# Gate and up products of two feed-forward layers as seven block products for eight

## The chip, the cores and the metric

The kernel runs on one core of one Trainium2 chip. The metric is the device time of one execution in microseconds (us). Each kernel runs several times; the median counts. The engines are called as the profile calls them: PE is TensorE (matmuls; PEld is its weight load), DVE is VectorE, ACT is ScalarE, POOL is GpSimd, and SP is SyncE, which issues the transfers.

## The reference: a two-layer trunk

Activations are 512 tokens by 1024 features in float32. Layer 0 mixes the tokens with multi-head latent attention, layer 1 with a gated linear recurrence. Around the mixer every layer does the same:

```
x <- LayerNorm(alpha * x + mixer(x))
x <- LayerNorm(alpha * x + SwiGLU(x))
x <- x + sigmoid(x W_gate[i]) * (p[i] W_proj[i])

def swiglu_ffn(x, w_in, w_down):
    h = x @ w_in                                # [512, 1024] @ [1024, 2 * 2816]
    g, u = h[..., :D_FF], h[..., D_FF:]         # D_FF = 2816 = 22 * 128
    return (jax.nn.silu(g) * u) @ w_down
```

The change concerns `x @ w_in`, the gate and up products, once in each layer.

## The kernel before, in words

**Exact products in three passes.** Every large operand is split into hi + lo (`split`, L104): ACT copies it to hi with fewer significant bits (L106), and DVE, or POOL where asked, subtracts hi from it to get lo (L107). `mm3` (L118) then issues three matmuls: hi·hi (L121), hi·lo (L122) and lo·hi (L123). A matmul takes 128 rows of contraction, 128 output features and as many columns as its name in the profile says. Weights come once from memory in units of 512 KB, a tile of 128 × 1024 (`unit`, L109: tiles `raw`, `whi`, `wlo`).

**Gate and up (`ffn`, L303).** D_FF is cut into 22 blocks of 128 features. For block j the unit of gate weights and that of up weights, 8 chunks of contraction each, go through `mm3` with all 512 tokens: 2 × 8 × 3 = 48 matmuls of 512 columns. ACT applies Silu to the gate bank (L315) and DVE multiplies it by the up bank (L316). Blocks 0 and 1 are done in two halves of 256 tokens: first both blocks for token tiles 0 and 1, then both for tiles 2 and 3. That is so because the activations are not ready yet.

**What stands ahead of it.** The mixer's output projection (`out_proj`, L289) makes x token tile by token tile (four tiles of 128 tokens), in two halves of 512 features. In the second half each tile's residual (L250), layer norm statistics (L256, L257, the Square on ACT at L258), the power on POOL (`rr`, L131) and two scaling steps (L263, L267) follow its matmuls; `flush` then transposes an earlier tile on PE (L227, bank `tp`) and splits it into the feature-major pair xT. The work of one tile is issued behind the matmuls of the next.

**What stands behind it.** `hT` holds the 22 blocks' results; the down projection splits one block of hT and one unit of weights at a time (`hsplit`, tiles `ma`), and multiplies into eight PSUM banks (`part`).

**What sets the order.** The code's text order is not the engines' order: a scheduler places each engine's instructions in one fixed list before the run, by tile pools and dependences. An engine works through its list in order, and an instruction that waits holds up all behind it. Tiles come from pools with a fixed number of buffers (`mid`: tags `ma`, 4 buffers, and `mb`, 5; `raw` 3, `whi` and `wlo` 5 each), and taking one again waits for its last reader. Large tiles come from `bigt`, six of 16 KB per partition.

Of the kernel before, what the change touches and what calls it, by code (L numbers as in the profile page):

```python
# [71 lines left out]


class Builder:
    def __init__(self, ctx, tc, ins, out):
# [19 lines left out]
    def bigt(self, shape, dt=F32):  # L95
        return self.big.tile(shape, dt, tag="big", name=self.nm("big"))
# [21 lines left out]
    def mm3(self, ps, a, b, start, stop):  # L118
        """ps += a^T b with (hi, lo) operands."""
        mm = self.nc.tensor.matmul  # L120
        mm(ps, a[0], b[0], start=start, stop=False)  # L121
        mm(ps, a[0], b[1], start=False, stop=False)  # L122
        mm(ps, a[1], b[0], start=False, stop=stop)  # L123
# [97 lines left out]
    def to_feat(self, src, dst, t, c0, n):  # L221
        """chunks c0..c0+n of src [128 tok, n*128] into dst hi/lo [128, chunk, tok]"""
        for g in range(0, n, 4):
            m = min(4, n - g)
            ps = self.bank("tp")
            for c in range(m):
                self.nc.tensor.transpose(out=ps[:, c * P:(c + 1) * P], in_=src[:, (g + c) * P:(g + c + 1) * P], identity=self.ident)  # L227
            sl = (slice(None), slice(c0 + g, c0 + g + m), slice(t * P, (t + 1) * P))
            self.split(dst[0][sl], dst[1][sl], ps.rearrange("p (c t) -> p c t", t=P)[:, :m])
# [592 lines left out]
```

## Time and profile before

| | |
|---|---|
| runs | 1330.73 to 1331.20 us, median 1331.07 |
| profiled execution | span 1329.1 us (its own time is not recorded apart from the span; the median of the runs lies 1.97 above it) |
| PE busy | 1305.8 us, 98% of the span |
| DVE, ACT, POOL busy | 640.2, 463.4, 85.6 us |
| gate/up of layer 0, first to last matmul | 187.28 to 430.88 us on the span's clock |
| moved by DMA | 124.74 MB, 94 GB/s on average |

How to read it: a line such as `L107 DVE TENSOR_TENSOR wlo<-raw,whi 128x1024 ... x195 | 240.3, 1235 | 261.5 <-ACT whi L106 256.9` is a group of 195 instructions of source line 107 on DVE that read `raw` and `whi` and write `wlo`; they were busy for 240.3 us, 1235 ns each on average; DVE was idle for 261.5 us just ahead of them, most of it until ACT's L106 was done. In a timeline the first two numbers are start and duration in us, and a bracket at the end is the idle time ahead. A clock of 1.00 is full speed for PE.

### The profile page before, as it was taken

How to read it: one execution, taken by the hardware profiler on the slowest of the kernel's cores; microseconds unless marked ns; L12 is line 12 of the kernel's file. 1: busy time of each engine (PE TensorE's matmuls, PEld its weight loads, DVE VectorE, ACT ScalarE, POOL GpSimd, SP SyncE). 2: the span in 40 equal slices, each digit the busy share in tenths (PEclk: the TensorE clock that was granted, in tenths of full speed). 3: DMA queues.
4: the chain of work that ended last, by engine and by line, in shares of the span. 5: the costliest groups of instructions: out<-in, count | busy, mean ns of one | idle time of the engine just before them, and what ended most of it. 6: DMA issues, size and time to landing. Idle time of an engine off the chain costs nothing.

```text
span 1329.1 us, 16105 instructions
## 1 busy us (share of the span) xinstructions
PE 1305.8 (98%) x6460; PEld 1094.5 (82%) x6460; DVE 640.2 (48%) x1068; ACT 463.4 (35%) x760; POOL 85.6 (6%) x87
## 2 busy tenths in 40 slices
PE   8999999999999999999999999999999999999998
PEld 8787889888888888788888887888888888888887
DVE  7988373322223333753367776456322222333473
ACT  6666243222222222542434344334222222233252
POOL 0200130000000000100002220023000000000000
PEclk9999989999999999999999999999999999999999
DMA  7212133233222222241311110314223232222221
GB/s 254 77 51 96 51 108 96 96 99 101 100 95 95 95 95 95 85 152 64 126 65 64 64 65 19 125 64 138 101 95 98 98 102 99 95 95 95 95 96 48
DMA packets 35932, 124.74 MB, mean 94 GB/s; under 512 B 4369, under 2 KB 4625, under 8 KB 35729
## 3 DMA queue, kind: packets, MB, share of 16 engines
q1 hardware_dynamic: 35856, 123.71, 27.9%
q8 instruction: 51, 0.84, 0.3%
q14 instruction: 25, 0.20, 0.0%
HBM read 121.60 MB, written 2.10 MB: 93 GB/s over the span
## 4 chain that ended last, share of the span: by engine, by line
PE 92%; DVE 5%; issue 1%; ACT 1%; POOL 1%; DMA 0%; SPq 0%; DVEq 0%; ACTq 0%; POOLq 0%
PE ps L122 24%; PE ps L121 24%; PE ps L123 23%; PE sc L121 2%; PE sc L122 2%; PE sc L123 2%; PE tp L121 2%; PE tp L122 2%; PE tp L123 2%; PE tp L227 2%; PE sc L658 2%; PE wg L122 1%; PE wg L123 1%; DVE big L267 1%; PE wg L121 1%
## 5 line engine op out<-in xcount | busy, mean ns | idle before, releaser
L106 ACT ACTIVATE whi<-raw 128x1024 fp32r<-128x1024 f32 (+1 forms) x215 | 224.0, 1043 | 438.3 <-PE ps L122 325.9
L107 DVE TENSOR_TENSOR wlo<-raw,whi 128x1024 fp32r<-128x1024 f32 (+1 forms) x203 | 246.4, 1216 | 262.5 <-ACT whi L106 257.9
L121 PE MATMUL ps<-big,whi 128*128 128x512 f32 (+1 forms) x928 | 351.4, 379 | 0.0
L123 PE MATMUL ps<-big,wlo 128*128 128x512 f32 (+1 forms) x928 | 350.6, 378 | 0.0
L122 PE MATMUL ps<-big,whi 128*128 128x512 f32 (+1 forms) x928 | 349.4, 377 | 0.0
L123 PEld LDWEIGHTS ps<-big,wlo 128*128 128x128 f32 x928 | 175.9, 190 | 30.5
L122 PEld LDWEIGHTS ps<-big,whi 128*128 128x128 f32 x928 | 176.0, 190 | 30.1
L121 PEld LDWEIGHTS ps<-big,whi 128*128 128x128 f32 x928 | 176.1, 190 | 29.4
L121 PE MATMUL ps<-whi,big 128*128 128x512 f32 (+2 forms) x440 | 171.0, 389 | 0.2 <-DVE ma L453 0.2
L123 PE MATMUL ps<-whi,big 128*128 128x512 f32 (+2 forms) x440 | 168.7, 383 | 0.0
L122 PE MATMUL ps<-wlo,big 128*128 128x512 f32 (+2 forms) x440 | 168.4, 383 | 0.0
L316 DVE TENSOR_TENSOR big<-ps,t 128x512 f32<-128x512 f32 (+1 forms) x48 | 31.1, 647 | 148.5 <-PE ps L123 148.5
L123 PEld LDWEIGHTS ps<-whi,big 128*128 128x128 f32 x440 | 83.1, 189 | 15.6
L121 PEld LDWEIGHTS ps<-whi,big 128*128 128x128 f32 x440 | 83.2, 189 | 14.6 <-ACT whi L106 0.4
L122 PEld LDWEIGHTS ps<-wlo,big 128*128 128x128 f32 x440 | 83.3, 189 | 14.5
L107 DVE TENSOR_TENSOR ma<-big,ma 128x512 fp32r<-128x512 f32 x44 | 30.4, 692 | 119.0 <-ACT ma L106 119.0
L131 POOL TENSOR_TENSOR rr<-rv,mhalf 128x1 f32<-128x1 f32 (+2 forms) x28 | 26.2, 934 | 912.2 <-DVE rv L129 912.2
L106 ACT ACTIVATE ma<-big 128x512 fp32r<-128x512 f32 x44 | 27.7, 631 | 140.4 <-PE wg L123 140.4
L123 PE MATMUL ps<-whi,ma 128*128 128x512 f32 x164 | 64.2, 391 | 0.0
L121 PE MATMUL ps<-whi,ma 128*128 128x512 f32 x164 | 64.2, 391 | 0.0
L122 PE MATMUL ps<-wlo,ma 128*128 128x512 f32 x164 | 64.0, 390 | 0.0
L106 ACT ACTIVATE big<-tp 128x512 fp32r<-128x512 f32 x52 | 29.8, 594 | 39.2 <-PE tp L227 39.1
(249 smaller groups left out, 1550.9 us busy)
## 6 DMA issues: line engine op xcount, KB each, us to landing
raw<-ffn_w_in SPq DMA_DIRECT2D x88, 512.0 KB, 3.3
raw<-ffn_w_down SPq DMA_DIRECT2D x44, 512.0 KB, 3.3
raw<-ple_w_gate SPq DMA_DIRECT2D x16, 512.0 KB, 3.3
raw<-hgrn_w_fq SPq DMA_DIRECT2D x16, 512.0 KB, 3.3
raw<-mla_w_o SPq DMA_DIRECT2D x8, 512.0 KB, 3.3
raw<-hgrn_w_v SPq DMA_DIRECT2D x8, 512.0 KB, 4.3
raw<-hgrn_w_g SPq DMA_DIRECT2D x8, 512.0 KB, 3.3
raw<-hgrn_w_o SPq DMA_DIRECT2D x8, 512.0 KB, 4.2
```

The source lines that it names most:

```text
L106: self.nc.scalar.activation(hi, src, AF.Copy)
L107: (eng or self.nc.vector).tensor_tensor(out=lo, in0=src, in1=hi.bitcast(F32), op=ALU.subtract)
L121: mm(ps, a[0], b[0], start=start, stop=False)
L122: mm(ps, a[0], b[1], start=False, stop=False)
L123: mm(ps, a[1], b[0], start=False, stop=stop)
L131: nc.gpsimd.tensor_tensor(out=r, in0=v, in1=self.mhalf[:, :n], op=ALU.pow)
L227: self.nc.tensor.transpose(out=ps[:, c * P:(c + 1) * P], in_=src[:, (g + c) * P:(g + c + 1) * P], identity=self.ident)
L267: v.scalar_tensor_tensor(out=xs, in0=xs, scalar=r, in1=gb[1][:, sl], op0=ALU.mult, op1=ALU.add)
L316: nc.vector.tensor_tensor(out=hT[j // 8][:, j % 8, lo:lo + n], in0=ps[1][:, :n], in1=g[:, :n], op=ALU.mult)
L658: nc.tensor.matmul(ps[:, c * P:(c + 1) * P], X[:, c * P:(c + 1) * P], pair_view(cs[0][:, :, 1, :], cs[1][:, :, 0, :]), start=True, stop=True)
```

## The change

Gate and up of a block together are a product of [512 tokens × 1024] with [1024 × (128 gate, 128 up)]. It is cut 2 × 2 × 2: tokens in halves of 256 (tiles 0, 1 and tiles 2, 3), the contraction in halves of 512, the outputs in gate and up. Eight half products become seven, in Winograd's form, at the cost of sums of weights and of activations ahead and of results behind.

- Activations: class `Winograd` holds A11, A12 (tiles 0, 1), A22 (tiles 2, 3) and the sums S1 to S4, hi and lo. `sink` takes a transposed tile: for t < 2 a split and a raw copy (L126), for t ≥ 2 a copy of A21 (L130), sums on DVE (L132, L137, L138) and POOL (L140), and three splits. S1 to S4 need tiles of both halves.
- Weights: `prep(j)` loads ra, the gate unit, and rb, the up unit (`lo` and `up` are the halves of the contraction in each), splits ra (h1, l1), forms `ta` on POOL (L389, L390, 512 wide each), `tb` on DVE (L391, L392), and splits rb's upper half (b22), ta (h2, l2) and tb (h3, l3).
- Products: seven of 4 chunks × 3 passes = 12 matmuls of 256 columns, in the order A11·B11 (bank A), S1·T1 (bank C), A12·B21 (bank B), S2·T2 (onto A), A22·T4, S4·B22 (onto C), S3·T3 (onto A). Between them ACT copies banks out (L416: g0, u1, u0, g1), DVE adds (L424 g0, L451 u0, L454 g1, L455 u1), ACT applies Silu (L425, L456) and POOL multiplies gate by up (L452, L457). In the text P1 and P2 are the products of A11 and A12.
- Blocks 0 and 1 are interleaved: A11 and A12 products of both, then A22, then the rest.
- hT of blocks 20 and 21 is a tile of pool `ma`; `ma` has 5 buffers for 4. All large tiles become 14 slots of 8 KB (`slot`, `Rows`, `Pair`), the layer norm parameters among them; x comes in two transfers instead of one. `split`, `mm3` and the layer norm stand at other lines (L178 and L179; L193 to L195; L318, L324 to L326, L331, L335; `rr` is L203, the transpose L297).

```diff
+    def sink(self, t, n, ps):
+        b, nc = self.b, self.b.nc
+        cs = slice(t % 2 * P, t % 2 * P + P)
+        if t < 2:
+            b.split(self.a1[0][:, n, :, cs], self.a1[1][:, n, :, cs], ps)
+            nc.scalar.activation(self.raw[n][:, :, cs], ps, AF.Copy)
+            return
+        if n == 0:
+            a21 = b.small([P, 4, P], tag="t2", bufs=T2)
+            nc.scalar.activation(a21, ps, AF.Copy)
+            sx = b.mid([P, 2, 4, P], tag="mb")
+            nc.vector.tensor_tensor(out=sx[:, 1], in0=self.raw[0][:, :, cs], in1=ps, op=ALU.subtract)
+            self.at[t] = a21, sx
+            return
+        a21, sx = self.at.pop(t)
+        sy = b.mid([P, 2, 4, P], tag="mb")
+        nc.vector.tensor_tensor(out=sx[:, 0], in0=ps, in1=a21, op=ALU.add)
+        nc.vector.tensor_tensor(out=sy[:, 0], in0=ps, in1=sx[:, 1], op=ALU.subtract)
+        b.split(self.a22[:, 0, :, cs], self.a22[:, 1, :, cs], ps)
+        nc.gpsimd.tensor_tensor(out=sy[:, 1], in0=self.raw[1][:, :, cs], in1=sy[:, 0], op=ALU.subtract)
+        b.split(self.s13[0][:, :, :, cs], self.s13[1][:, :, :, cs], sx)
+        b.split(self.s24[0][:, :, :, cs], self.s24[1][:, :, :, cs], sy)
...
+    def gate_up(self, l, xT):
...
+        def prep(j):
+            ra, rb = (self.wp.tile([P, 1024], F32, tag="raw", bufs=3, name=self.nm("raw")) for _ in range(2))
+            nc.sync.dma_start(ra, win[j, 0])
+            nc.sync.dma_start(rb, win[j, 1])
...
+            self.split(h1, l1, ra)
+            ta, tb = self.mid([P, 1024]), self.mid([P, 1024])
+            lo, up = slice(0, 512), slice(512, 1024)
+            nc.gpsimd.tensor_tensor(out=ta[:, up], in0=rb[:, up], in1=rb[:, lo], op=ALU.subtract)
+            nc.gpsimd.tensor_tensor(out=ta[:, lo], in0=rb[:, lo], in1=ra[:, lo], op=ALU.subtract)
+            v.tensor_tensor(out=tb[:, lo], in0=ta[:, up], in1=ra[:, lo], op=ALU.add)
+            v.tensor_tensor(out=tb[:, up], in0=tb[:, lo], in1=ra[:, up], op=ALU.subtract)
+            b22 = self.mid([P, 2, 512], F32R)
+            self.split(b22[:, 0], b22[:, 1], rb[:, up])
...
+            self.split(h2, l2, ta)
+            h3, l3 = self.mid([P, 1024], F32R, "mb"), self.mid([P, 1024], F32R, "mb")
+            self.split(h3, l3, tb)
...
+        def block(j):
+            w = prep(j)
+            if j < 20 and j % 4 == 0:
+                hT.append(self.slot([P, 4, S]))
+            elif j == 20:
+                hT.append(self.mid([P, 2, S]))
...
+            product(A, xT("A11"), w["B11"])
+            copy(g0, A)
...
+            product(C, xT("S1"), w["T1"])
+            copy(u1, C)
+            if j >= 2:
+                p2()
+            product(A, xT("S2"), w["T2"], True)
+            copy(u0, A)
+            if j >= 2:
+                g1 = p4()
+            product(C, xT("S4"), w["B22"], True)
+            v.tensor_tensor(out=u0, in0=C[:, :N], in1=u0, op=ALU.add)
+            nc.gpsimd.tensor_tensor(out=h[:, :N], in0=u0, in1=g0, op=ALU.mult)
+            product(A, xT("S3"), w["T3"], True)
+            v.tensor_tensor(out=g1, in0=A[:, :N], in1=g1, op=ALU.subtract)
+            v.tensor_tensor(out=u1, in0=A[:, :N], in1=u1, op=ALU.add)
+            nc.scalar.activation(g1, g1, AF.Silu)
+            nc.gpsimd.tensor_tensor(out=h[:, N:], in0=u1, in1=g1, op=ALU.mult)
+            yield
...
     def ffn(self, l, x, xT, ln):
-        nc = self.nc
-        hT = [self.bigt([P, 8, S]), self.bigt([P, 8, S]), self.bigt([P, 6, S])]
-        NB = 2
...
-        ws = [[self.unit(win[j, q], True) for q in range(2)] for j in range(NB)]
-        for lo in (0, 256):
-            for j in range(NB):
-                block(j, ws[j], lo, 256)
-                self.flush()
-        for j in range(NB, NF):
-            block(j, [self.unit(win[j, q]) for q in range(2)], 0, 512)
-
+        hT = self.gate_up(l, xT)
```

POOL at the entry of layer 0's feed-forward part, before: the powers `rr` of token tiles 0, 1, 2 and 3, and the lo splits of the units of blocks 0 and 1.

```order
L107 TENSOR_TENSOR wlo_2096<-raw_2093,whi_2095 128x1024
L131 TENSOR_TENSOR rr_1928<-rv_1926,mhalf 128x1
L131 TENSOR_TENSOR rr_1980<-rv_1978,mhalf 128x1
L131 TENSOR_TENSOR rr_2032<-rv_2030,mhalf 128x1
L107 TENSOR_TENSOR wlo_2102<-raw_2099,whi_2101 128x1024
L107 TENSOR_TENSOR wlo_2108<-raw_2105,whi_2107 128x1024
L107 TENSOR_TENSOR wlo_2114<-raw_2111,whi_2113 128x1024
L131 TENSOR_TENSOR rr_2084<-rv_2082,mhalf 128x1
```

The same place after: `rr` of tiles 0 to 3 at L203, the weight differences of blocks 0 and 1 at L389 and L390, and the activation sums of tiles 2 and 3 at L140.

```order
L203 TENSOR_TENSOR rr_1944<-rv_1942,mhalf 128x1
L203 TENSOR_TENSOR rr_1998<-rv_1996,mhalf 128x1
L389 TENSOR_TENSOR ma_2128<-raw_2121 128x512
L390 TENSOR_TENSOR ma_2128<-raw_2121,raw_2120 128x512
L389 TENSOR_TENSOR ma_2208<-raw_2201 128x512
L390 TENSOR_TENSOR ma_2208<-raw_2201,raw_2200 128x512
L203 TENSOR_TENSOR rr_2052<-rv_2050,mhalf 128x1
L140 TENSOR_TENSOR mb_2097<-ma_1752,mb_2097 128x512
L203 TENSOR_TENSOR rr_2114<-rv_2112,mhalf 128x1
```

The differences of blocks 0 and 1 now stand between `rr` of tile 1 and `rr` of tile 2; before, three splits stood between tile 2's and tile 3's.

DVE in the middle of gate/up, before: two lo splits and one multiplication (L316) a block, three blocks shown.

```order
L107 TENSOR_TENSOR wlo_453_2612<-raw_451_2609,whi_452_2611 128x1024
L316 TENSOR_TENSOR big_383_2090<-ps_437_2486,t2_438_2535 128x512
L107 TENSOR_TENSOR wlo_459_2671<-raw_457_2668,whi_458_2670 128x1024
L107 TENSOR_TENSOR wlo_462_2677<-raw_460_2674,whi_461_2676 128x1024
L316 TENSOR_TENSOR big_383_2090<-ps_446_2551,t2_447_2600 128x512
```

After, one round of block 6's additions with the weight work of blocks 8 and 9 between them: l1 and g0, l2, l3, the lower half of tb, u0, the upper half of tb, b22's lo, g1, u1 (`sc`, `ps` are PSUM banks, `part` the copies of them).

```order
L179 TENSOR_TENSOR wlo_563_3183<-raw_560_3178,whi_562_3182 128x1024
L424 TENSOR_TENSOR part_535_2947<-sc_534_2946,part_535_2947 128x256
L179 TENSOR_TENSOR wlo_568_3196<-ma_564_3186,whi_567_3195 128x1024
L179 TENSOR_TENSOR mb_570_3200<-ma_565_3187,mb_569_3199 128x1024
L391 TENSOR_TENSOR ma_585_3317<-ma_584_3316,raw_580_3308 128x512
L451 TENSOR_TENSOR part_537_2962<-ps_536_2961,part_537_2962 128x256
L392 TENSOR_TENSOR ma_585_3317<-ma_585_3317,raw_580_3308 128x512
L179 TENSOR_TENSOR ma_586_3322<-raw_581_3309,ma_586_3322 128x512
L454 TENSOR_TENSOR part_540_3017<-ps_533_2945,part_540_3017 128x256
L455 TENSOR_TENSOR part_538_2963<-ps_533_2945,part_538_2963 128x256
```

Three instructions a block became ten, and weight work and additions for PE's current block alternate in one list.

POOL at the end of gate/up, after; before, it has nothing there. `ma_802` is hT of blocks 20 and 21, and `ma_815` is ta of block 21.

```order
L452 TENSOR_TENSOR big_725_4237<-part_787_4642,part_785_4627 128x256
L457 TENSOR_TENSOR big_725_4237<-part_788_4643,part_790_4697 128x256
L452 TENSOR_TENSOR ma_802_4754<-part_807_4772,part_805_4757 128x256
L389 TENSOR_TENSOR ma_815_4867<-raw_812_4860 128x512
L390 TENSOR_TENSOR ma_815_4867<-raw_812_4860,raw_811_4859 128x512
L457 TENSOR_TENSOR ma_802_4754<-part_808_4773,part_810_4827 128x256
```

The weight differences of block 21 stand behind the multiplication L452 of block 20, which needs that block's u0; in the middle of gate/up they stand some two blocks ahead of their use.

More of the change, by code (lines that the diff above doesn't have):

```diff
@@ L71, in pair_view, with __init__, __call__ @@
     return bass.AP(u.tensor, u.offset, [u.ap[0], (v.offset - u.offset, 2), *u.ap[1:]])
+class Rows:
+    def __init__(self, b, dt=F32):
+        self.z = [b.slot([P, 2, D], dt) for _ in range(NT // 2)]
+    def __call__(self, t, cols=slice(None)):
+        return self.z[t // 2][:, t % 2, cols]
+class Pair:
+    def __init__(self, b):
+        self.b = b
+        self.z = [[b.slot([P, 4, S], F32R) for _ in range(2)] for _ in range(KC // 4)]
+    def __call__(self, kc, cols=slice(None)):
+        return [z[:, kc % 4, cols] for z in self.z[kc // 4]]
+    def sink(self, t, n, ps):
+        hi, lo = (z[:, :, t * P:(t + 1) * P] for z in self.z[n])
+        self.b.split(hi, lo, ps)
@@ new lines, with __init__, __call__, sink @@
+class Winograd:
+    def __init__(self, b):
+        self.b = b
+        two = lambda: [b.slot([P, 2, 4, 256], F32R) for _ in range(2)]
+        self.a1, self.s13, self.s24 = two(), two(), two()
+        self.a22 = b.slot([P, 2, 4, 256], F32R)
+        self.raw = [b.mid([P, 4, 256]) for _ in range(2)]
+        self.at = {}
+    def __call__(self, name):
+        if name == "A22":
+            return self.a22[:, 0], self.a22[:, 1]
+        z, n = {"A11": (self.a1, 0), "A12": (self.a1, 1), "S1": (self.s13, 0), "S3": (self.s13, 1),
+                "S2": (self.s24, 0), "S4": (self.s24, 1)}[name]
+        return z[0][:, n], z[1][:, n]
+    def sink(self, t, n, ps):
+        b, nc = self.b, self.b.nc
[19 more added lines that the diff above has]
+        b.split(self.s24[0][:, :, :, cs], self.s24[1][:, :, :, cs], sy)
@@ L78, in __init__ @@
         self.cst = pool("cst", bufs=1)
-        self.big = pool("big", bufs=6)
+        self.big = pool("big", bufs=SLOTS)
         self.wp = pool("wp", bufs=5)
@@ L93, in bank, with slot @@
         return self.ps.tile([P, 512], F32, tag=tag, bufs=PSUM_BUFS[tag], name=self.nm(tag))
[L95 to L96 removed]
+    def slot(self, shape, dt=F32):
+        return self.big.tile(shape, dt, tag="big", bufs=SLOTS, name=self.nm("big"))
     def mid(self, shape, dt=F32, tag="ma"):
@@ L218, in lower_bounds, with to_feat @@
         v.tensor_scalar(out=self.oml, in0=self.lb, scalar1=-1.0, scalar2=1.0, op0=ALU.mult, op1=ALU.add)
[L221 to L229, printed above, removed]
+    def to_feat(self, src, sink, t, n):
+        ps = self.bank("tp")
+        for c in range(4):
+            self.nc.tensor.transpose(out=ps[:, c * P:(c + 1) * P], in_=src[:, c * P:(c + 1) * P], identity=self.ident)
+        sink(t, n, ps.rearrange("p (c t) -> p c t", t=P))
     def defer(self, *args):
@@ L363, in ple @@
         self.split(pT[0], pT[1], praw)
-        pp = self.bigt([P, NT, D])
-        yT = None if last else self.pair()
+        pp = Rows(self)
+        yT = None if last else Pair(self)
         for n in range(2):
@@ L434, in mla @@
         kr = self.mid([P, NT, ROPE])
-        cb = self.bigt([P, 2, 4, S], F32R)
-        cT = (cb[:, 0], cb[:, 1])
+        cT = [self.slot([P, 4, S], F32R) for _ in range(2)]
+        csink = lambda t, n, ps: self.split(*(z[:, :, t * P:(t + 1) * P] for z in cT), ps)
         cns = []
```

179 lines of the change are left out of this document (107 added, 72 removed).

## The prediction, made before the changed kernel ran

> **What bounds the kernel now.** I read the page first: busy time, the clock row, the chain that ended last, the DMA issues.
>
> ```profile
> PE 1305.8 (98%) x6460; PEld 1094.5 (82%) x6460; DVE 640.2 (48%) x1068; ACT 463.4 (35%) x760; POOL 85.6 (6%) x87
> ...
> PEclk9999989999999999999999999999999999999999
> ...
> PE 92%; DVE 5%; issue 1%; ACT 1%; POOL 1%; DMA 0%; SPq 0%; DVEq 0%; ACTq 0%; POOLq 0%
> ...
> raw<-ffn_w_in SPq DMA_DIRECT2D x88, 512.0 KB, 3.3
> ```
>
> TensorE bounds it nearly everywhere; VectorE idles half of the time and GpSimd nearly all of it. Fewer matmul columns are therefore worth something, as long as the additions that buy them stay hidden. A matmul's duration overlaps the next one's, so its price must come from starts: the timeline of PE (start, duration, operation; in brackets the idle time ahead), from layer 0's last projection tile to its first down-projection matmul. After it, the same engine by stretches (busy us and count for PE, PEld, DVE, ACT, POOL; then the clock).
>
> ```profile
> 182.58 0.39 PE L123 MATMUL ps<-whi,big 128*128 128x512 f32 x1
> 183.79 0.63 PE L227 MATMUL tp<-ident,big 128*128 128x128 f32 x4 [0.82 <-DVE big L267]
> 186.54 1.09 PE L227 MATMUL tp<-ident,big 128*128 128x128 f32 x4 [2.12 <-DVE big L267]
> 187.28 0.56 PE L121 MATMUL ps<-big,whi 128*128 128x256 f32 x1
> ...
> 196.32 0.28 PE L122 MATMUL ps<-big,whi 128*128 128x256 f32 x1
> ...
> 213.47 0.40 PE L121 MATMUL ps<-big,whi 128*128 128x512 f32 x1
> ...
> 430.88 0.39 PE L123 MATMUL ps<-big,wlo 128*128 128x512 f32 x1
> 431.10 0.39 PE L121 MATMUL tp<-whi,ma 128*128 128x512 f32 x1
> ```
>
> ```profile
> 186.00:192.00 6.00, 5.46 (x26) 5.49 (x27) 5.82 (x11) 2.79 (x4) 3.61 (x2) 0.50 0.49 175
> ...
> 196.00:212.00 16.00, 16.00 (x136) 16.00 (x135) 5.40 (x9) 5.62 (x9) 0.00 (x0) 1.00 0.27 86
> ...
> 240.00:260.00 20.00, 20.00 (x90) 16.55 (x89) 6.28 (x6) 5.21 (x6) 0.00 (x0) 1.00 0.24 85
> ```
>
> Blocks 2 to 21 are 20 × 48 = 960 matmuls of 512 columns from 213.47 to 431.10: 0.2267 us each, 10.88 us a block. From 196.32 to 213.47 stand 143 matmuls of 256 columns: 0.120 us each. So 256 columns cost 53% of 512, not 50%. After the idle times of 0.82 and 2.12 us the clock is 0.50 for 6 us, which costs about 3 us.
>
> The prices of the other engines' work, by shape (count, then busy us, mean ns of one), one group from each kind:
>
> ```profile
> L107 DVE TENSOR_TENSOR wlo<-raw,whi 128x1024 fp32r<-128x1024 f32 x195 | 240.3, 1235 | 261.5 <-ACT whi L106 256.9
> L107 DVE TENSOR_TENSOR big<-tp,big 128x512 fp32r<-128x512 f32 x52 | 34.3, 685 | 4.2 <-ACT big L106 4.2
> L107 DVE TENSOR_TENSOR mb<-tp,mb 128x256 fp32r<-128x256 f32 x32 | 13.2, 416 | 0.9 <-ACT mb L106 0.7
> ...
> L106 ACT ACTIVATE whi<-raw 128x1024 fp32r<-128x1024 f32 x207 | 218.5, 1057 | 433.2 <-PE ps L122 325.9 <-issue 47.5 <-PE ps L123 36.3
> L106 ACT ACTIVATE big<-tp 128x512 fp32r<-128x512 f32 x52 | 29.8, 594 | 39.2 <-PE tp L227 39.1
> L106 ACT ACTIVATE mb<-tp 128x256 fp32r<-128x256 f32 x32 | 11.8, 384 | 2.8 <-DVE mb L107 2.2 <-PE tp L551 0.2
> ...
> L258 ACT ACTIVATE t<-big,lnst 128x1024 bf16<-128x1024 f32 x16 | 18.4, 1149 | 21.4 <-DVE lnst L257 21.4
> ...
> L671 POOL TENSOR_TENSOR mb<-mb 128x256 f32<-128x256 f32 x4 | 2.5, 613 | 0.3
> ```
>
> How GpSimd and VectorE get along is seen in the timelines of both, at three places: the tail of the layer norm (first seven rows), a quiet one and two crossings elsewhere.
>
> ```profile
> 173.25 1.00 POOL L131 TENSOR_TENSOR rr<-rv,mhalf 128x1 f32<-128x1 f32 x1 [4.74 <-DVE rv L129]
> 180.55 8.07 POOL L107 TENSOR_TENSOR wlo<-raw,whi 128x1024 fp32r<-128x1024 f32 x3
> ...
> 174.41 1.41 DVE L267 SCALAR_TENSOR_TENSOR big<-big,rr,lnb 128x512 f32<-128x512 f32 x2
> 177.60 0.15 DVE L257 TENSOR_SCALAR lnst<-lnst 128x1 f32<-128x1 f32 x1
> 180.75 5.65 DVE L267 SCALAR_TENSOR_TENSOR big<-big,rr,lnb 128x512 f32<-128x512 f32 x2
> 186.32 0.68 DVE L250 SCALAR_TENSOR_TENSOR big<-big,ps 128x512 f32<-128x512 f32 x1
> 187.04 1.60 DVE L256 TENSOR_TENSOR lnst<-lnst 128x1 f32<-128x1 f32 x1
> ...
> 676.48 1.21 POOL L671 TENSOR_TENSOR mb<-big 128x512 f32<-128x512 f32 x1 [111.93 <-DVE big L634]
> ...
> 714.15 2.35 POOL L671 TENSOR_TENSOR mb<-ma 128x512 f32<-128x512 f32 x1 [1.70 <-DVE ma L634]
> ...
> 714.37 1.22 DVE L107 TENSOR_TENSOR wlo<-raw,whi 128x1024 fp32r<-128x1024 f32 x1
> ...
> 50.40 0.74 POOL L400 TENSOR_TENSOR ma<-ma 128x256 f32<-128x256 f32 x1 [1.71 <-issue]
> ...
> 50.51 0.42 DVE L399 TENSOR_TENSOR ma<-ps,mb 128x256 f32<-128x256 f32 x1
> ```
>
> A pair of L267 takes 1.41 us alone and 5.65 us beside GpSimd's subtractions; they take turns, one whole instruction each. GpSimd's 512-wide L671 takes 1.21 us alone and 2.35 us beside a 1.22 us VectorE split. VectorE with one PSUM operand (L399, L250) is not disturbed. So all that VectorE and GpSimd do from SBUF on both operands is serial.
>
> **The change, part by part.**
>
> *Matmuls of blocks 2 to 21.* Seven products of 12 make 84 × 0.120 = 10.08 us for 10.88: −0.80 us a block, −16.0 us a layer, −32 us in all; 7.4%, not the eighth of the arithmetic. [...]
>
> *What a block adds beside them.* VectorE: three 1024-wide subtractions, three 512 wide, four 256 wide from PSUM: 3 × 1.235 + 3 × 0.685 + 4 × 0.416 = 7.4 us. ACT: three of 1.057, one of 0.594, six of 0.384: 6.1 us. GpSimd: 2 × 1.21 + 2 × 0.613 = 3.6 us. Each fits into 10.08 us. But they hang together in a ring that runs round once per block, in the order shown above: h2 (1.06), l2 (1.24; L389 of the next block waits for the buffer that l2 reads), L389 (1.21), l3 (1.24), L390 (1.21), L391 (0.69), L451 (0.42), L452 (0.61), L392 (0.69), b22's lo (0.69), L454 (0.42), then on ACT Silu, copy g0, copy u1 (0.38 each), and h2 again. That is 10.6 us; without L452, where VectorE goes first, 10.0; some 0.4 less for neighbours on one engine that overlap. So 9.6 to 10.6 us. A second ring is the weight tile rb, held once: its transfer waits for b22's lo and takes 3.3 us, and L389 waits for it: 6.7 + 3.3 = 10.0 us. Both lie at the matmuls' 10.08. I take 10.15 a block, near the middle: 20 × 0.73 = −14.6 us a layer. Ends: 10.08 (−16.0) and 10.6 (−5.6).
>
> *The entry*, per layer, on the clock above. Before, tile 2's and tile 3's layer norm hide behind 11.5 us of products on tiles 0 and 1 (two blocks × 48 × 0.120); afterwards only P1 and P2 of both blocks are there, 4 × 12 × 0.120 = 5.8 us, and all else needs tiles 2 and 3.
> - L389 and L390 of block 0 alternate with tile 1's second layer norm step, L335 (L267 before): 174.4 + 1.4 + 2 × 1.2 less overlaps, so it ends near 178.1, not 175.8. PE's transposes of tile 1 wait 1.0 us for it, and the last projection tile ends at 184.1, not 183.0.
> - Tile 2's statistics then stand behind its residual, L391, b22's lo, L392 and tile 1's two splits: 178.1 + 6 × 0.69 = 182.2, not 177.6. Its Square (1.15) stands on ACT behind h2 and the two raw copies (to 183.7) and ends at 185.0. Its rr stands on POOL behind L389 and L390 of block 1, which wait for l2 (184.3) and take turns with L331: 184.3 + 2 × 1.21 + 0.7, and 1.0 for rr, 188.4. L335 ends near 189.8 (before 186.4): PE, which has 11 matmuls of P1 to put there (1.3 us), idles some 3.7 us.
> - Tile 3's statistics stand behind one 1024-wide and three 512-wide operations of VectorE (194.4), its Square behind h3 and two splits (196.6), its scaling among 1024-wide splits: L335 ends near 201.5. PE has done P1 and P2 by 195, at half clock.
> - The A22 hi half follows at 206.5, behind L132, L137, L138 and the raw copy.
> - Ten products are left: 14.4 us, 2 more for the clock. Block 2 starts near 223, before at 213.47: **+9.5 us a layer**. Nearest bounds: +4 if ACT and VectorE hide half of this line, +15 if each step slips by another 1.1 us.
>
> *The exit.* hT of blocks 20 and 21 takes a buffer of pool `ma`, so block 21's weight work starts only behind block 20's L452 (the third order listing). From the end of block 20's S4·B22: u0 0.4, L452 to 1.1, L389 2.3, L390 3.5, h2 4.6; on VectorE L391, L454, L455, L392, b22's lo and L457's turn, l2 to 8.0, l3 to 9.7. PE's first S1·T1 is due at 2.9 and gets h2 at 4.6; the lo part waits to 8.0, and S2·T2 starts at 9.4 where 5.8 was due: +3.4 us. These stalls are about as long as those which brought the clock to 0.50 above, and six us at that cost 3; I take half, 1.3. **+4.7 us a layer**, bounds +1 and +7. [...]
>
> *The rest.* Two x transfers for one, the layer norm's parameters in slots, later places of a few transfers: zero, as PE's chain passes none of them; cover is a whole stage of matmuls (over 20 us) each. Slots of 8 KB: bounds 0 and ±1 us.
>
> **Sum.** Per layer −14.6 + 9.5 + 4.7 = −0.4; two layers −0.8. The span of 1329.1 becomes 1328.3. The runs' median, 1331.07, stands 1.97 above the profiled span; with that left as it is, **1330 us**: no change that could be told, since about 0.2%, 2.7 us, is what a measurement tells here.
>
> **The rivals.**
> R1, everything is hidden: the block keeps 10.08, blocks 0 and 1 save 24 × 0.120 = 2.9 us, and no stall is added: −18.9 a layer, 1293 us. With half of my entry and exit left, −16.0 + 7.1 a layer: 1313. For it: idle time of VectorE and ACT. Against it: tile 3's layer norm already left PE idle 2.12 us with the longer cover.
> R2, VectorE and GpSimd pace the blocks: since they take turns, all of their work in series is 5.8 + 3.6 + 1.7 = 11.1 us a block. At 10.6, where the ring closes without overlap, 40 × 0.45 = +18: 1348 us; at 11.1, 1368. It decides from 10.2 on, where the gain of the blocks no longer pays for entry and exit.
> R3, the entry alone goes deeper: with three stalls of 3.7 us and more the clock stays at 0.50 over the ten products, 10 to 14 us instead of 2: 1342 to 1350.
>
> **How the numbers follow.** My forecast, each term near its size, 1322 to 1339: 0.42 (0.18 faster, 0.15 same, 0.09 slower). R1, 1293 to 1318: 0.22, faster. R2: 0.20, 0.19 of it slower. R3: 0.14, 0.13 of it slower, 0.01 same. Another: 0.02, mostly faster. That gives 0.43, 0.17 and 0.40. The range leaves out R1's lower half and R2's upper half: 1310 to 1350.
>
> **What would show it.** Windows of blocks 5 to 15: 84 matmuls of 256 columns in 10.1 to 10.2 us, clock 1.00; at 10.08 the ring is slack, at 10.6 PE waits for L451 or ACT's copy g0 each block. GpSimd L389 means of 1.2 to 2.4 us and L391 or l3 waiting for it. Entry: PE waits for L335 twice for over 3 us, and for the A22 split; S1·T1 some 24 us after the last projection matmul. Exit: PE waiting for h2 and l2 of block 21. The prediction is wrong if stalls at the entry are under half of this, or if the block strays from 10.15 by over 0.3 us, which alone is 12 us.

## The result and the profile after

The changed kernel took 1347.73 us (median of 4 runs, 1346.86 to 1348.93), the kernel before 1331.13 (1330.73 to 1331.23) beside it: 1.0128 of the time, 95% interval 1.0113 to 1.0142. It is 16.6 us slower. The profiled span went from 1329.1 to 1345.2 us, +16.1.

The page of the changed kernel, in the order in which the page before was read:

```profile
PE 1286.0 (96%) x7852; PEld 1144.8 (85%) x7852; DVE 905.9 (67%) x1396; ACT 615.2 (46%) x1080; POOL 328.3 (24%) x259
...
PE 82%; DVE 9%; issue 3%; POOL 3%; ACT 2%; DMA 1%; SPq 0%; DVEq 0%; POOLq 0%; ACTq 0%
...
raw<-ffn_w_in SPq DMA_DIRECT2D x88, 512.0 KB, 3.6
```

PE is busy 20 us less, yet the span is 16 us longer: PE's share of the chain fell from 92% to 82%, and DVE, POOL, ACT and "issue" have it now. PE's waits over the whole run (for whom, us in total, times, longest):

```profile
PE tp L297 <- DVE big L335: 15.8, 6, 4.2
PE ps L193 <- ACT part L416: 7.4, 4, 2.6
PE ps L193 <- ACT big L178: 6.0, 2, 3.3
PE tp L193 <- ACT whi L178: 5.7, 1, 5.7
PE ps L193 <- DVE part L451: 5.6, 4, 1.9
PE ps L193 <- ACT whi L178: 4.0, 2, 2.0
PE ps L194 <- DVE big L179: 2.5, 2, 1.3
```

The fourth is the wait at the start of the program that the kernel before has too (5.3 us there). L335 and the A22 splits (big L178, big L179) belong to the entry; L416 and L451 are copies and additions of single blocks; the whi in the last line but one is h2 of block 21. The same waits in time, layer 0, PE's timeline:

```profile
177.85 0.63 PE L297 MATMUL tp<-ident,big 128*128 128x128 f32 x4 [0.95 <-DVE big L335]
188.61 0.92 PE L297 MATMUL tp<-ident,big 128*128 128x128 f32 x4 [3.35 <-DVE big L335]
200.07 1.94 PE L297 MATMUL tp<-ident,big 128*128 128x128 f32 x8 [4.16 <-DVE big L335]
204.67 0.58 PE L193 MATMUL ps<-big,whi 128*128 128x256 f32 x1 [2.65 <-ACT big L178]
206.99 0.58 PE L194 MATMUL ps<-big,whi 128*128 128x256 f32 x1 [1.25 <-DVE big L179]
226.98 0.39 PE L193 MATMUL ps<-big,whi 128*128 128x256 f32 x1 [1.47 <-DVE part L451]
236.84 0.58 PE L193 MATMUL ps<-big,whi 128*128 128x256 f32 x1 [2.64 <-ACT part L416]
244.51 0.39 PE L193 MATMUL ps<-big,mb 128*128 128x256 f32 x1 [0.28 <-ACT part L416]
254.10 0.38 PE L193 MATMUL ps<-big,whi 128*128 128x256 f32 x1 [1.94 <-DVE part L451]
427.84 0.58 PE L193 MATMUL ps<-big,whi 128*128 128x256 f32 x1 [2.01 <-ACT whi L178]
438.18 0.40 PE L193 MATMUL tp<-whi,ma 128*128 128x512 f32 x1
```

Five waits belong to the entry, four to blocks 2, 3 and 4, one to the exit. Between 254.10 and 425.55 there is none. Counting 168 matmuls from the entry on, block 2 starts at 223.7 us (before 213.47); the down projection starts at 438.18 (before 431.10), so layer 0 loses 7.1 us, and layer 1 the other 9.0 of the span's 16.1 (from one layer's down projection to the other's: 724.2 us, before 715.1). The windows of PE (busy us and count for PE, PEld, DVE, ACT, POOL, then the clock), the undisturbed stretch of layer 0 first, then the three us behind the wait of 2.64 and those behind the wait of 2.01:

```profile
260.00:420.00 160.00, 160.00 (x1335) 160.00 (x1335) 131.62 (x150) 87.29 (x153) 89.77 (x60) 1.00 0.31 95
...
237.50:240.50 3.00, 3.00 (x18) 3.00 (x18) 1.15 (x3) 1.39 (x2) 1.34 (x2) 0.58 0.74 298
...
428.50:431.50 3.00, 3.00 (x16) 2.84 (x16) 2.70 (x5) 2.27 (x3) 0.61 (x1) 0.56 0.47 162
```

1335 matmuls in 160 us are 0.120 us each, 10.07 us for the 84 of a block: the arithmetic of the change works, in the blocks that run undisturbed.

| us a layer | forecast | layer 0 | layer 1 |
|---|---|---|---|
| entry, to the start of block 2 | +9.5 | +10.2 | +12.3 |
| blocks 2 to 21 at their matmuls' pace | −16.0, with the ring −14.6 | −16.0 | −16.0 |
| exit, block 21 | +4.7 | +4.0 | +3.7 |
| blocks 2 to 4, starting stalls | 0 | +8.9 | +9.1 |
| sum | −0.4 | +7.1 | +9.1 |

The rows are counted from the starts of the blocks, 84 matmuls each. In layer 0 block 2 takes 15.9 us, block 3 11.0 and block 4 12.3, each of blocks 5 to 20 10.08, and block 21 14.1.

How the largest of the starting stalls comes about is read from the timelines of POOL, DVE, ACT and of SP's queue ahead of 236.84:

```profile
228.93 1.53 POOL L457 TENSOR_TENSOR big<-part,part 128x256 f32<-128x256 f32 x1 [0.26 <-ACT part L456]
230.42 2.28 POOL L389 TENSOR_TENSOR ma<-raw 128x512 f32<-128x512 f32 x1
232.66 1.29 POOL L390 TENSOR_TENSOR ma<-raw,raw 128x512 f32<-128x512 f32 x1
239.16 1.29 POOL L389 TENSOR_TENSOR ma<-raw 128x512 f32<-128x512 f32 x1 [5.21 <-DMA raw<-ffn_w_in]
...
229.78 1.77 DVE L179 TENSOR_TENSOR wlo<-raw,whi 128x1024 fp32r<-128x1024 f32 x1
...
233.98 1.06 ACT L178 ACTIVATE whi<-ma 128x1024 fp32r<-128x1024 f32 x1 [3.45 <-POOL ma L390]
235.46 1.06 ACT L178 ACTIVATE mb<-ma 128x1024 fp32r<-128x1024 f32 x1
236.43 0.37 ACT L416 ACTIVATE part<-ps 128x256 f32<-128x256 f32 x1
...
226.14 0.33 SPq L383 DMA_DIRECT2D raw<-ffn_w_in  x1
235.58 0.33 SPq L383 DMA_DIRECT2D raw<-ffn_w_in  x1
```

PE needs the copy u0 of block 2 (ACT, 236.43). It stands in ACT's list behind h2 and h3 of block 4; h2 idled 3.45 us for POOL's L390; L390 stands behind L389, which took 2.28 us in turns with DVE (1.29 at 239.16, where DVE idles) and could start only when POOL had done the multiplication L457 ahead of it, at 230.46. Its rb, sent for at 226.14, when DVE had released that tile, took 3.7 us and so was there 0.6 us before that. In the next round the tile decides: the next rb goes out at 235.58, and POOL's next L389 idles 5.21 us for it. So three things are in these stalls: the turns, the lists, and the tile rb that is sent for late.

### The profile page after: what moved, and what is told of

It reads as the page before. It is cut to its first block, busy times and chain, and to the rows that moved or that the text cites. A ratio compares the mean times of both kernels' runs of the same rounds, so it can differ in the third digit from the quotient of the medians.

```text
span 1345.2 us, 20010 instructions
## 1 busy us (share of the span) xinstructions
PE 1286.0 (96%) x7852; PEld 1144.8 (85%) x7852; DVE 905.9 (67%) x1396; ACT 615.2 (46%) x1080; POOL 328.3 (24%) x259
## 4 chain that ended last, share of the span: by engine, by line
PE 82%; DVE 9%; issue 3%; POOL 3%; ACT 2%; DMA 1%; SPq 0%; DVEq 0%; POOLq 0%; ACTq 0%
PE ps L194 18%; PE ps L193 18%; PE ps L195 18%; PE sc L193 3%; PE sc L194 3%; PE sc L195 3%; PE wg L194 3%; PE wg L195 3%; PE wg L193 3%; PE tp L297 2%; DVE wlo L179 2%; PE sc L803 2%; PE tp L195 1%; PE tp L193 1%; PE tp L194 1%
## 5 line engine op out<-in xcount | busy, mean ns | idle before, releaser
L179 DVE TENSOR_TENSOR wlo<-raw,whi 128x1024 fp32r<-128x1024 f32 (+1 forms) x167 | 204.7, 1228 | 83.2 <-ACT whi L178 81.2
L193 PE MATMUL ps<-big,whi 128*128 128x256 f32 (+1 forms) x688 | 217.7, 316 | 20.8 <-ACT big L178 6.0
L178 ACT ACTIVATE whi<-raw 128x1024 fp32r<-128x1024 f32 (+1 forms) x171 | 177.1, 1038 | 111.2 <-PE ps L194 52.2
L195 PE MATMUL ps<-big,wlo 128*128 128x256 f32 (+1 forms) x688 | 216.5, 315 | 1.2 <-DVE wlo L179 1.2
L194 PE MATMUL ps<-big,whi 128*128 128x256 f32 (+1 forms) x688 | 215.1, 313 | 2.5 <-DVE big L179 2.5
L193 PE MATMUL ps<-whi,big 128*128 128x512 f32 (+2 forms) x440 | 171.0, 389 | 0.0
L195 PE MATMUL ps<-whi,big 128*128 128x512 f32 (+2 forms) x440 | 168.7, 383 | 0.0
L193 PEld LDWEIGHTS ps<-big,whi 128*128 128x128 f32 x688 | 133.8, 194 | 28.1 <-ACT big L178 6.6
L194 PEld LDWEIGHTS ps<-big,whi 128*128 128x128 f32 x688 | 133.7, 194 | 8.5 <-DVE big L179 3.1
L195 PEld LDWEIGHTS ps<-big,wlo 128*128 128x128 f32 x688 | 133.7, 194 | 6.8 <-DVE wlo L179 1.6
L203 POOL TENSOR_TENSOR rr<-rv,mhalf 128x1 f32<-128x1 f32 (+2 forms) x28 | 26.8, 958 | 424.7 <-DVE rv L201 424.7
L195 PEld LDWEIGHTS ps<-whi,big 128*128 128x128 f32 x440 | 83.1, 189 | 15.5
L179 DVE TENSOR_TENSOR ma<-big,ma 128x512 fp32r<-128x512 f32 x40 | 28.5, 717 | 100.4 <-ACT ma L178 100.4
L193 PEld LDWEIGHTS ps<-whi,big 128*128 128x128 f32 x440 | 83.2, 189 | 14.3
L390 POOL TENSOR_TENSOR ma<-raw,raw 128x512 f32<-128x512 f32 x44 | 87.8, 1994 | 0.0
L179 DVE TENSOR_TENSOR mb<-ma,mb 128x1024 fp32r<-128x1024 f32 x44 | 76.8, 1744 | 15.0 <-PE wg L194 15.0
L178 ACT ACTIVATE ma<-big 128x512 fp32r<-128x512 f32 x40 | 25.2, 630 | 122.6 <-PE wg L195 120.4
L389 POOL TENSOR_TENSOR ma<-raw 128x512 f32<-128x512 f32 x44 | 60.9, 1383 | 79.3 <-DVE wlo L179 63.4
L391 DVE TENSOR_TENSOR ma<-ma,raw 128x512 f32<-128x512 f32 x44 | 65.6, 1490 | 19.1 <-POOL ma L389 16.6
L457 POOL TENSOR_TENSOR big<-part,part 128x256 f32<-128x256 f32 x40 | 59.7, 1493 | 54.8 <-ACT part L456 54.8
```

What stands on the lines that cost most here:

```text
L178: self.nc.scalar.activation(hi, src, AF.Copy)
L179: (eng or self.nc.vector).tensor_tensor(out=lo, in0=src, in1=hi.bitcast(F32), op=ALU.subtract)
L193: mm(ps, a[0], b[0], start=start, stop=False, skip_group_check=more)
L194: mm(ps, a[0], b[1], start=False, stop=False, skip_group_check=more)
L195: mm(ps, a[1], b[0], start=False, stop=stop, skip_group_check=more)
L203: nc.gpsimd.tensor_tensor(out=r, in0=v, in1=self.mhalf[:, :n], op=ALU.pow)
```

## The experiments

All totals are medians beside runs of the kernel before on the same chip (1330.4 to 1331.1). "Starting stalls" are PE's waits from the start of block 2 to about 260 us (265 where block 5 still has one), layer 0: 6.3 us in the changed kernel; by the blocks' lengths, with restarts and half clock, they cost 8.9. S and C are theories on the entry: S is that turns and list positions of weight work make it long, C that the lost cover does.

**Where the differences are made.** First, both on DVE:

```diff
-            nc.gpsimd.tensor_tensor(out=ta[:, up], ...)
-            nc.gpsimd.tensor_tensor(out=ta[:, lo], ...)
+            v.tensor_tensor(out=ta[:, up], ...)
+            v.tensor_tensor(out=ta[:, lo], ...)
```

> The two weight differences L389 and L390 of every block go from GpSimd to VectorE; all else stays. Theory S (VectorE and GpSimd take turns, and GpSimd's differences stand ahead of the layer norm's power and of VectorE's additions): the waits for L335 fall from 0.95, 3.35 and 4.16 us to about 0, 1.5 and 3.5, the stalls of blocks 2 to 4 (6.3 us in layer 0, 6.6 in layer 1) fall below 2; about -14 us, 1334. Theory C (the cover: only 5.8 us of products are free of token tiles 2 and 3): the entry keeps all but 1 us of its stalls; only the stalls of blocks 2 to 4 can go, 1338 to 1346. If VectorE gets too full (7.4 + 1.4 = 8.8 of 10.08 us a block): PE waits for it in every block, above 1350.

1337.36 us, −10.4. The starting stalls fell to 0.8, as S had it; block 2 starts at 219.2, 4.5 earlier; but the waits for L335 became one of 6.04 us, so most of the entry stays, as C had it. In return DVE sets the pace in blocks 5 to 17 or so: PE waits 0.35 us for L451 in each, and they are 10.79 us apart. PE's timeline, two of them:

```profile
284.20 0.39 PE L193 MATMUL ps<-big,whi 128*128 128x256 f32 x1 [0.35 <-DVE part L451]
...
294.99 0.39 PE L193 MATMUL ps<-big,whi 128*128 128x256 f32 x1 [0.34 <-DVE part L451]
```

The same for blocks 0 and 1 alone (`v if j < 2 else nc.gpsimd`):

> L389 and L390 go to VectorE for blocks 0 and 1 alone, so that GpSimd has no weight work ahead of the layer norm's powers. Theory S: entry 3 us shorter per layer, the stalls of blocks 2 to 4 as before: 1342. Theory C: within 2 us of 1347.7, since VectorE still has the same serial work.

1344.64 us, −3.1, between the two. Block 2 starts at 220.4, 3.3 us earlier, as S had it, but the starting stalls rose to 8.1 (the last, 1.94 us, at 263.29): they are no leftover of the entry.

One of the two on DVE (L390), L389 on GpSimd, else as changed:

> The changed kernel with one edit: L390 on VectorE, L389 still on GpSimd. If GpSimd's pair of differences causes the starting stalls of blocks 2 to 4, one of the two leaves them at 2 to 4 us a layer (6.3 and 6.6 in the changed kernel), VectorE has 8.1 of 10.08 us and the blocks stay at 10.08, and the entry gains 1 to 2 us of the 4.5 that block 2's start gained with both differences on VectorE: 1347.7 - 5 to 12, about 1339. If the starting stalls come from the late entry alone, they stay above 5 us: 1344 or more.

1334.50 us, −13.2: one line, and four fifths of the loss, more than expected. The starting stalls are 3.8 us, block 2 starts at 220.7, and the later blocks keep 10.08. In layer 0 the gain is 3.0 us at the entry, 3.2 in the starting blocks and 1.0 at the exit.

GpSimd's multiplications on DVE, the differences on GpSimd (`h[:, :N]` and `h[:, N:]` by `v`):

> The changed kernel with GpSimd's two multiplications L452 and L457 on VectorE, the differences L389 and L390 still on GpSimd. Theory order (GpSimd's differences stand behind a multiplication that waits for Silu, and so all behind them slip): the stalls of blocks 2 to 4 fall from 6.3 and 6.6 us to below 3, total -6 to -8, 1340. Theory turns (the differences themselves take 1.3 to 2.3 us instead of 1.2 beside VectorE): the stalls stay above 4 us a layer, total within 4 us of 1347.7.

1350.00 us, +2.3. The starting stalls halved to 3.3 in layer 0, so the multiplications on GpSimd have a part in them. But from then on PE waits 0.17 us for DVE in almost every block, and they are 10.56 us apart; by the blocks' lengths that costs 6.7 us in layer 0, against 2.1 won in blocks 2 to 4 and 3.6 at the exit. Neither theory had that.

**The exit.** hT of blocks 20 and 21 in two tiles of pool `t2`:

```diff
-                hT.append(self.mid([P, 2, S]))
+                hT.append([self.small([P, S], tag="t2", bufs=T2) for _ in range(2)])
```

> hT of blocks 20 and 21 is two tiles of the pool that holds Silu's results elsewhere, instead of one of pool ma, so that block 21's weight differences need not wait for block 20. If the buffer is the cause of the exit's stall, the waits for h2 and l2 of block 21 (2.0 us in layer 0, 2.0 and 1.2 in layer 1) go, and the half clock of 3.4 us behind them in layer 0 with them (1.7 us): -5 to -7 us, 1341 to 1343. If another wait takes its place: no change.

1338.98 us, −8.75, more than expected. PE has no wait at the exit any more, the clock is 1.00 there, and the down projection starts 4.1 us earlier:

```profile
434.12 0.40 PE L193 MATMUL tp<-whi,ma 128*128 128x512 f32 x1
```

Layer 1 gave as much: its down projection starts at 1154.24 for 1162.38, 8.1 us earlier over both layers. The buffer was the cause.

**The entry.** Blocks 0 and 1 as before the change:

```diff
-        first = [block(0), block(1)]
+        ws = [[self.unit(win[j, q], True) for q in range(2)] for j in range(2)]
+        for n in range(2):
+            a = [xT("A11"), xT("A12")] if n == 0 else [xT("A21"), xT("A22")]
+            for j in range(2):     # gate and up, 8 chunks each, 256 tokens
...
```

> Blocks 0 and 1 are done as before the change (gate and up units, two halves of 256 tokens, eight half products), the sums for blocks 2 to 21 as in the changed kernel; A21 is split too. Theory C: 11.5 us of products on token tiles 0 and 1 hide tile 2 and 3 again; block 2 starts at 214 to 217 us instead of 223.9, and its sums have 11.5 us more: stalls of blocks 2 to 4 below 3 us. -7 to -10 per layer for the entry and -3 to -6 for the start: 1316 to 1328. Theory S: the sums and splits in line on VectorE delay tile 3 as much as before; block 2 starts after 219, and the total stays above 1335.

1333.14 us, −14.6. Block 2 starts at 215.1, 8.6 us earlier, which is where C put it. Its second half fails: with 8 us more time the starting stalls are still 6.2 us. So the late entry is not the cause of the starting stalls. That the lost cover is most of the entry is likely, but not shown alone: this kernel also does without the weight sums of blocks 0 and 1, and moving two of them off GpSimd was worth 3.3 us above.

**All together, and what is left.** With blocks 0 and 1 as before and own buffers for hT, the differences both on DVE, both on GpSimd, one on each:

> Three edits together: blocks 0 and 1 as before the change, hT of blocks 20 and 21 in buffers of their own, L389 and L390 of all blocks on VectorE. If the three causes lie one behind the other in time, their gains add: 1347.7 - 14.6 - 8.75 - 10.4 = 1314. If the first and the third take the same stalls away (the first two blocks no longer have L389 and L390 ahead of the layer norm): 1316 to 1322. VectorE's ring of 10.4 to 10.8 us a block, seen when L389 and L390 stood on it, would remain and keep it above 1312.

> Blocks 0 and 1 as before the change and hT of blocks 20 and 21 in buffers of their own; L389 and L390 stay on GpSimd. Gains add: 1333.1 - 8.75 = 1324.4. The stalls of blocks 2 to 4 (6 us a layer) stay if GpSimd's turns are their cause, and vanish if they came from the late entry: then below 1316.

> As the one before, but L390 on VectorE and L389 on GpSimd. If a round's length is set by how many whole instructions take turns, one on each engine gives blocks at 10.08 us and starting stalls of 2 to 3 us a layer: 1314 to 1318. If one GpSimd difference is enough to hold up VectorE and ACT in line, it stays where the one before is: 1324.

1317.62, 1327.49 and 1308.87 us; the last, faster than any figure expected for it, is 0.9837 of the kernel before (0.9823 to 0.9852). The first has no starting stall, and DVE's ring at 10.79 us in blocks 7 to 19 (its price seen alone: 9.3 us a layer). The second has starting stalls of 7.3 us, the third of 3.0, and both run at 10.08 behind them, but for one block of the second. The other half of the pair on DVE, and two more edits to the third kernel:

> Blocks 0 and 1 as before the change, hT of blocks 20 and 21 in buffers of their own, and the pair split the other way: L389 on VectorE, L390 on GpSimd. If only the number of whole instructions in turn matters: within 3 us of 1308.9. If what matters is that GpSimd's L389 waits for a buffer that VectorE's l2 reads and then holds up VectorE's L391 (which needs L389's result), then this kernel has no such wait on GpSimd's side and is faster: 1300 to 1306.

> The 1308.9 us kernel (blocks 0 and 1 as before, hT of 20 and 21 in buffers of their own, L390 on VectorE) with the lo splits of blocks 0 and 1 on VectorE instead of GpSimd, where each takes 2.4 us and stands in turn with the layer norm's steps. If turns cause the layer norm's waits there (1.03 and 4.04 us in layer 0): they fall to 0 and about 2.5, -3 to -5 us in all: 1304 to 1306. If VectorE's own queue (splits, sums) is what tile 3 waits for, four more splits of 1.2 us on it make it slower: 1309 to 1313.

> The 1308.9 us kernel with the second of GpSimd's two multiplications (0.6 us alone, 1.5 us beside VectorE) on VectorE. If its turn lies in the round that sets the start: stalls of blocks 2 to 4 (3.0 us in layer 0) below 2: 1305 to 1307. If not, VectorE gets 0.4 to 0.7 us more a block, still below 10.08: within 2 us of 1308.9.

1309.99, 1308.57 and 1309.31 us: none can be told from 1308.87. For the mirrored pair, the wait on GpSimd's side is thus not what matters. In the second, block 2 starts at 210.5 instead of 213.5 and the layer norm's waits of 1.03 and 4.04 us became one of 1.39, as turns would have it, but the starting stalls rose to 5.3 and ate it.

**Turns, result or transfer.** In the 1308.87 kernel GpSimd does L390 a second time, into a tile that nobody reads:

```diff
             v.tensor_tensor(out=ta[:, lo], in0=rb[:, lo], in1=ra[:, lo], op=ALU.subtract)
+            nc.gpsimd.tensor_tensor(out=self.small([P, 512], tag="t2", bufs=T2), in0=rb[:, lo], in1=ra[:, lo], op=ALU.subtract)
```

> The 1308.9 us kernel (L389 on GpSimd, L390 on VectorE), in which GpSimd does L390 too, into a tile that nobody reads. Theory turns (GpSimd's whole instructions delay VectorE's, whoever needs the result): the starting stalls return and the total goes to 1320 to 1335, near or above the kernel with both on GpSimd (1327.5). Theory result (VectorE and ACT wait for GpSimd's second result, turns cost little): within 4 us of 1308.9.

1335.95 us, +27.1. VectorE's own L390, source line 394 in both, by shape: first without the idle work (1308.87), then with it.

```profile
L394 DVE TENSOR_TENSOR ma<-raw,raw 128x512 f32<-128x512 f32 x40 | 32.4, 811 | 2.3 <-DMA raw<-ffn_w_in 1.3
```

```profile
L394 DVE TENSOR_TENSOR ma<-raw,raw 128x512 f32<-128x512 f32 x40 | 58.3, 1458 | 2.9 <-DMA raw<-ffn_w_in 1.9
```

0.81 became 1.46 us; the starting stalls are 7.2, and PE waits some 0.3 us in each later block, 10.6 us apart. So another instruction on GpSimd costs time though nobody waits for its result. How much of that is turns is not shown: the idle work also stands ahead of the next L389 in GpSimd's list, and it reads both weight tiles, which can be given back only when it is done.

Four tiles `raw` for three, paid for with a buffer of `mb`, and the buffer alone as its control:

```diff
-MID_BUFS = {"ma": 5, "mb": 5}
+MID_BUFS = {"ma": 5, "mb": 4}
...
-            ra, rb = (self.wp.tile([P, 1024], F32, tag="raw", bufs=3, ...
+            ra, rb = (self.wp.tile([P, 1024], F32, tag="raw", bufs=4, ...
```

> The changed kernel with four weight tiles raw instead of three, paid for with one buffer less of pool mb (the next kernel has that alone). Theory transfers (the starting stalls come from rb's transfer, which waits for VectorE's b22 lo before it): with a tile to spare the transfers come earlier and the stalls of blocks 2 to 4 fall from 6.3 and 6.6 us below 3 a layer: -8 to -12, 1336 to 1340. Theory turns: they stay above 5, within 3 us of the next kernel.

> The changed kernel with four buffers of pool mb instead of five; the control for the kernel before. h3 and l3 and the sums of tiles 2 and 3 live there: 1347.7 if a buffer was to spare, up to 1355 if the sums must wait for one.

1331.45 and 1338.64 us. The tile is worth 7.2 us, and the starting stalls fall from 4.6 (control) to 0.5. GpSimd's L389 idles for rb's transfer 33 times in the control (also in later blocks, where PE does not wait for it), 4 times in the changed kernel, and never with the fourth tile. So in the control the transfer has the larger part in the stalls. That it has it in the changed kernel too is likely, but not shown; and with the fourth tile the scheduler also exchanged a few rows on ACT, DVE and GpSimd between 200 and 230 us, whose worth is not separated. All that is left of the stalls with the fourth tile, in PE's timeline:

```profile
227.54 0.39 PE L193 MATMUL ps<-big,mb 128*128 128x256 f32 x1 [0.28 <-ACT part L416]
...
238.39 0.39 PE L193 MATMUL ps<-big,mb 128*128 128x256 f32 x1 [0.22 <-ACT part L416]
```

The surprise is the control: a buffer less is 9.1 us faster. SP's list is unchanged by it and GpSimd's nearly so, but ACT's and DVE's are not: in the later blocks h3 on ACT, and L451, L392 and b22's lo on DVE, stand in another order, and at the start the copy u0 of block 2 stands ahead of block 4's h3 on ACT. With that the wait of 2.64 us became 1.47:

```diff
 L178 ACTIVATE whi_2678<-ma_2669 128x1024
 L425 ACTIVATE part_2430<-part_2430 128x256
+L416 ACTIVATE part_2445<-ps_2428 128x256
 L178 ACTIVATE mb_2682<-ma_2670 128x1024
-L416 ACTIVATE part_2445<-ps_2428 128x256
 L416 ACTIVATE part_2500<-wg_2487 128x256
```

Both edits, the fourth tile and the buffer less, in three of the better kernels (one difference on each engine; both on GpSimd; one on each and the lo splits of blocks 0 and 1 on DVE):

> The 1308.9 us kernel with four tiles raw and four buffers of mb. If the late transfer of rb makes what is left of the starting stalls (3.0 us in layer 0), they fall below 1 a layer: 1301 to 1306. If turns make it: within 3 us of 1308.9.

> The 1327.5 us kernel (both differences on GpSimd) with four tiles raw and four buffers of mb. If the transfer is the cause and the turns only make it late, the spare tile takes the starting stalls (7.3 us in layer 0) below 1.5 here too: 1308 to 1314. If turns are a cause of their own, they stay above 4: 1320 or more.

> The 1308.6 us kernel (lo splits of blocks 0 and 1 on VectorE too) with four tiles raw and four buffers of mb. Its block 2 starts 3 us earlier than the 1308.9 us kernel's, and its starting stalls ate that up; if the spare tile removes them it is the fastest: 1298 to 1304; if VectorE's backlog makes them: 1306 to 1309.

1307.99, 1309.32 and **1297.80 us**; the last is 0.9754 of the kernel before (0.9740 to 0.9769), the fastest of all. The second gains most: with both differences on GpSimd the two edits take 18.2 us off (1327.49 to 1309.32), and the starting stalls fall from 7.3 to 2.5. No run has the buffer alone there, so the tile's own part is not known; in the changed kernel it was 7.2 of 16.3. The first shows the limit: its starting stalls fell from 3.0 to 1.4, but the wait for the layer norm rose from 4.0 to 4.7 us, and the total hardly moved: that is what the turns were expected to give, though the stalls halved. In the third the starting stalls fell from 5.3 to 2.3 and the wait for the layer norm from 1.39 to 0.27, and nothing but small waits is left; the largest over the whole run, after the start:

```profile
PE ps L197 <- ACT part L420: 2.8, 4, 1.6
PE ps L197 <- DVE part L455: 2.2, 2, 1.1
```

## Why the prediction was wrong

Its range held the time, its direction did not: no change was forecast, and it was 1.3% slower. That the range held is luck: its upper part stood there for R2 and R3, and neither is what happened.

- **Matmul prices: right.** 0.120 us for 256 columns, −16.0 us a layer in blocks 2 to 21.
- **The entry: right in its waits, its size in part by luck.** In layer 0 the waits for L335 were 0.95 and 3.35 us (forecast 1.0 and 3.7), tile 3's L335 was awaited until 200.07 (201.5), A22's hi until 204.67 (206.5), and block 2 started at 223.7 (223). The split thus came 1.8 us early, but the ten products behind it took 19.0 us for 16.4, since the clock was 0.50 for the first 8 us and PE waited 1.25 us more for the split's lo. In layer 1 the entry cost 12.3 us for 9.5. The changed kernel is not slower there (39.4 us from its first gate/up matmul to block 2, in layer 0 39.9); the kernel before is 2.2 us quicker (24.0 for 26.2). For the half clock which the prediction had read behind 0.82 and 2.12 us of idling was there in layer 0 alone: behind the same two waits in layer 1 the clock stayed at 1.00 (rows in the last section).
- **The exit: right in its cause, near in size.** Block 21 took 4.0 and 3.7 us more, against 4.7, and buffers of its own took away 4.1 in each layer. The parts were others than forecast (3.4 of waiting and 1.3 of clock): 2.0 us of waiting with half clock behind it in layer 0, 3.2 us at full clock in layer 1.
- **The ring: the step that failed.** "I take 10.15 a block, near the middle" spread one period over all of blocks 2 to 21, and so put +1.4 us a layer on the ring. In fact the ring is slack where it runs (10.08 us a block), and blocks 2 to 4, where the lists are not yet in that order, stall PE by 6.3 and 6.6 us, which with what hangs on it (restarts and half clock) costs 8.9 and 9.1. Of the 16.9 us by which the span missed its forecast, some 15 are this term. The second ring, rb "held once", had been named, and its 10.0 us set against 10.08 as if that were enough; with a buffer of `mb` less, the fourth tile and the row exchanges that came with it took the stalls from 4.6 to 0.5. Taking turns has a part too: L390 took 1.99 us on average against 1.27 at its shortest, and one difference fewer on GpSimd left 3.8 us of the 6.3. The prediction's "all that VectorE and GpSimd do from SBUF on both operands is serial" is wider than what ran: in the kernel before, `rr` (128x1) ran its 1.00 us at 173.25 beside a pair of L263 (128x512), and none of the 32 L263 took more than 0.75 us.
- The prediction's own signs of being wrong did not see it: its windows were to be blocks 5 to 15, and these ran as they should.
- R2 (engines pace the blocks) was not what happened, though the kernels with both differences on DVE show that it is near: their period is 10.79. R3 (a deeper entry) and R1 (all hidden) did not happen.

Open is how the 8.9 us split between turns, lists and transfer: they are links of one chain, and shortening any of them shortens the stalls. Why DVE with 8.8 us of work needs 10.79 a block was not settled.

## What to carry to other kernels

A ring that is just slack in the steady state can still have its price in its first rounds: look at the first blocks and the last one by themselves, list by list, and try a spare for the tile that closes the ring. Trading PE work for additions on other engines paid here when the first blocks kept work that needs none of them. The form of seven products for eight went from 1.3% slower to 2.5% faster with blocks 0 and 1 as before, own buffers for hT at the exit, a fourth weight tile for one buffer of `mb`, and with one difference a block and the lo splits of blocks 0 and 1 on DVE instead of GpSimd. And count on the lists: one buffer less reordered ACT's and DVE's rows and won 9 us that nobody had expected; which of the rows did it was not isolated.
